# A fourth block product in each gate and up group, and three low parts made by an accumulating DMA

## The chip, the cores and the metric

The kernel runs on one core of one Trainium2 chip. The metric is device time in microseconds of one execution. The core's engines work side by side and wait for each other on semaphores: TensorE (PE) multiplies matrices into PSUM, VectorE (DVE) and ScalarE (ACT) work element by element, GpSimd (POOL) does small side work and issues a few DMAs, and SyncE (SP) issues the loads of the weights.

## The reference, cut to what matters

The model has two layers over a residual stream of 256 tokens and 2048 features. Each layer is a normed mixer and then a normed SwiGLU feed-forward network, and a last norm ends it. All weights and data are float32. The change lies in the feed-forward network:

```python
FFN_HIDDEN = -(-(8 * D_MODEL) // (3 * 256)) * 256      # 5632

def swiglu(xn, w_gate, w_up, w_down):
    return (jax.nn.silu(xn @ w_gate) * (xn @ w_up)) @ w_down
...
        h = h + swiglu(rms_norm(h, norm_ffn[layer]), w_gate[layer], w_up[layer], w_down[layer])
```

So `xn` is 256 x 2048, gate and up are 2048 x 5632 each, and down is 5632 x 2048.

## The kernel before, in words

Every float32 operand `a` is split into a high part `hi`, rounded to float32r, and a low part `lo = a - hi`. A product is three matmuls into one PSUM bank: high by high, high by low, low by high (`three`, lines 350 to 353, or lines 173 to 175 in the plain loop). A weight tile has 128 rows of k and 512 columns. Two k rows of tiles make a *pair* and are loaded with one DMA of 512 KB into a `raw` tile (`load_raw`, line 94, all on SP's queue, in order). `split_chunk` (line 147) then makes `hi` with a cast on ACT (line 150) and `lo` with a subtraction on DVE (line 151). `hi` and `lo` are rings of 6 buffers, the plain `raw` tiles a ring of 4. PE thus consumes a chunk of 512 KB in 2 (k rows) x 2 (blocks of 128 tokens) x 3 = 12 matmuls.

The feed-forward network (`ffn`, line 419) walks over the 5632 hidden columns in 11 *groups* of 512, in three *blocks* of 3, 4 and 4 groups (`PARTS`). A group computes gate and up for its 512 columns over all 2048 rows of k, that is 8 pairs, then the gated product, then four transposes per token block into `pf` (line 450), which give the left operand of down. After each block, the part of down that needs these columns is computed and added to the residual stream.

`pair_group` (line 358) computes a group for two matrices at once. `ORDER` gives its 8 pairs in sequence; a 0 marks a *plain* pair, a 1 a *block product*. A plain pair is 4 half products for each matrix, 24 matmuls, from two chunks (gate, then up). A block product takes the 2 x 2 blocks (two token blocks by two k rows, and two k rows by two matrices) with seven products in place of eight, 21 matmuls. It needs sums of the left operand, made beforehand while x is split (`sums_of`, line 208, called from `split_scaled` for every pair in `mixed_of(ORDER)`), and sums of the weights: four differences `t4` (lines 386 to 389, DVE), which are split into `ht` (ACT) and `lt` (DVE) in two halves (line 397). It also needs gate's chunk split (`hg`, `lg`) and the second row of up split (`hu`, `lu`, line 392). Four of the seven products go to four `prod` banks, shared by all block products of the group; three go straight to the plain banks. At the end of the group DVE combines the `prod` banks into `c` (lines 412 to 416) and adds the plain banks (line 438).

The buffers of a block product: `raw` tiles of the pool `fp`, two (one for gate, one for up); `t4`, one; `ht` and `lt`, two each, and both are used by one product. In `ORDER` of before, the three block products of a group are the pairs 2, 3 and 6, with a plain pair between any two.

The program is written in the order of the mathematics, but a scheduler that works when the program is built decides the order in which each engine gets its instructions. On the chip each engine then runs its list strictly in order. The same `pair_group` computes down, with the orders in `DOWN`.

Of the kernel before, what the change touches and what calls it, by code (L numbers as in the profile page):

```python
# [7 lines left out]
F32 = mybir.dt.float32  # L8
F32R = mybir.dt.float32r
AF = mybir.ActivationFunctionType  # L10
ALU = mybir.AluOpType
# [4 lines left out]
P = 128  # L16
# [5 lines left out]
NB = 512  # L22
CK = 2
# [7 lines left out]
OFF_QM, OFF_KM, OFF_VM, OFF_OM = 1536, 2048, 2560, 3584  # L31
CAP = 15.0
FILL = 24
ORDER = ((0, 0), (0, 1), (1, 2), (0, 4), (1, 3), (0, 5), (1, 6), (0, 7))
DOWN = {
    6: ((0, 0), (0, 1), (1, 2), (0, 3), (0, 4), (0, 5)),
    8: ((0, 0), (0, 1), (1, 2), (0, 3), (0, 4), (1, 5), (0, 6), (0, 7)),
# [11 lines left out]
def trunk(  # L49
# [20 lines left out]
    nc = tc.nc  # L70
# [7 lines left out]
    wr = ctx.enter_context(tc.tile_pool(name="wr", bufs=4))  # L78
# [12 lines left out]
    gn = [cp.tile([2 * KT, P], F32, name=f"gn{i}") for i in range(2)]  # L91
    nc.scalar.dma_start(gn[0], norm_mix.rearrange("l (k p) -> (l k) p", p=P))

    def load_raw(w, k0, c0, n, pool=wr):
        raw = pool.tile([P, CK, NB], F32, tag="raw", name="raw")
        nc.sync.dma_start(
            raw[:, :, 0:n], w[k0 * P : (k0 + CK) * P, c0 : c0 + n].rearrange("(k p) n -> p k n", p=P)
        )
        return raw
# [5 lines left out]
    for n in range(4):  # L105
# [7 lines left out]
        out=ident, in_=ident, pattern=[[-1, P]], compare_op=ALU.not_equal, fill=1.0, base=0, channel_multiplier=1  # L113
# [5 lines left out]
        out=upper, in_=ones, pattern=[[1, P]], compare_op=ALU.is_ge, fill=0.0, base=0, channel_multiplier=-1  # L119
# [20 lines left out]
    gain_columns(0)  # L140


    def load_chunk(w, k0, c0, n):
        raw = ahead.pop(0) if ahead else load_raw(w, k0, c0, n)
        return split_chunk(raw, n)

    def split_chunk(raw, n):
        hi = wp.tile([P, CK, NB], F32R, tag="hi", name="hi")
        lo = wp.tile([P, CK, NB], F32R, tag="lo", name="lo")
        nc.scalar.copy(hi[:, :, 0:n], raw[:, :, 0:n])  # L150
        nc.vector.tensor_tensor(  # L151
            out=lo[:, :, 0:n], in0=raw[:, :, 0:n], in1=hi[:, :, 0:n].bitcast(F32), op=ALU.subtract
        )
        return hi, lo
# [34 lines left out]
    sums = {}  # L189
# [55 lines left out]
    def split_plain(dst_h, dst_l, src):  # L245
        nc.scalar.copy(dst_h, src)  # L246
        nc.vector.tensor_tensor(out=dst_l, in0=src, in1=dst_h.bitcast(F32), op=ALU.subtract)  # L247
# [107 lines left out]
    def bank(par, name):  # L355
        return pm.tile([P, NB], F32, tag="pm", name=name) if par else pa.tile([P, NB], F32, tag="acc", name=name)

    def pair_group(fp, par, lhs, sums, mats, order):
        plain = [[bank(par, "acc") for _ in range(NT)] for _ in range(2)]
        prods = None  # L360
        kinds = [kind for kind, _ in order]
        t0, t1 = slice(0, P), slice(P, 2 * P)
        for pos, (kind, pair) in enumerate(order):
            k0 = 2 * pair
            if not kind:
                last = pos == len(order) - 1
                walk = [(i, t) for i in range(CK) for t in range(NT)]
                if last:
                    walk.sort(key=lambda it: it[1])
                for m, (w, c0) in enumerate(mats):  # L370
                    hi, lo = load_chunk(w, k0, c0, NB)
                    for i, t in walk:
                        ah, al = lhs(k0 + i)
                        ts = slice(t * P, (t + 1) * P)
                        three(
                            plain[m][t], ah[:, ts], al[:, ts], hi[:, i, :], lo[:, i, :],
                            pos == 0 and i == 0, last and i == CK - 1,
                        )
                continue
            first, last = 1 not in kinds[:pos], 1 not in kinds[pos + 1 :]  # L380
            if first:
                prods = [bank(1 - par, "prod") for _ in range(4)]
            ra, rb = (load_raw(w, k0, c0, NB, fp) for w, c0 in mats)
            hg, lg = split_chunk(ra, NB)
            t4 = fp.tile([P, 4, NB], F32, tag="t4", name="t4", bufs=1)
            nc.vector.tensor_tensor(out=t4[:, 0, :], in0=rb[:, 0, :], in1=ra[:, 0, :], op=ALU.subtract)
            nc.vector.tensor_tensor(out=t4[:, 1, :], in0=rb[:, 1, :], in1=rb[:, 0, :], op=ALU.subtract)
            nc.vector.tensor_tensor(out=t4[:, 2, :], in0=rb[:, 1, :], in1=t4[:, 0, :], op=ALU.subtract)
            nc.vector.tensor_tensor(out=t4[:, 3, :], in0=ra[:, 1, :], in1=t4[:, 2, :], op=ALU.subtract)
            hu = wp.tile([P, CK, NB], F32R, tag="hi", name="hi")  # L390
            lu = wp.tile([P, CK, NB], F32R, tag="lo", name="lo")
            split_plain(hu[:, 1, :], lu[:, 1, :], rb[:, 1, :])
            ht, lt = [], []
            for i in range(2):
                hs = fp.tile([P, 2, NB], F32R, tag="ht", name="ht")
                ls = fp.tile([P, 2, NB], F32R, tag="lt", name="lt")
                split_plain(hs, ls, t4[:, 2 * i : 2 * i + 2, :])
                ht += [hs[:, 0, :], hs[:, 1, :]]
                lt += [ls[:, 0, :], ls[:, 1, :]]
            sh, sl = sums(pair)  # L400
            xa, la = lhs(k0)
            xb, lb = lhs(k0 + 1)
            three(prods[0], xa[:, t0], la[:, t0], hg[:, 0, :], lg[:, 0, :], first, last)
            three(plain[0][0], xb[:, t0], lb[:, t0], hg[:, 1, :], lg[:, 1, :], False, False)
            three(plain[1][0], sh[:, 3, :], sl[:, 3, :], hu[:, 1, :], lu[:, 1, :], False, False)
            three(prods[1], sh[:, 0, :], sl[:, 0, :], ht[0], lt[0], first, last)
            three(prods[2], sh[:, 2, :], sl[:, 2, :], ht[1], lt[1], first, last)
            three(prods[3], sh[:, 1, :], sl[:, 1, :], ht[2], lt[2], first, last)
            three(plain[0][1], xb[:, t1], lb[:, t1], ht[3], lt[3], False, False)
        c = fp.tile([P, 4, NB], F32, tag="c", name="c", bufs=1)  # L410
        u2 = fp.tile([P, NB], F32, tag="tmp", name="u2")
        nc.scalar.copy(c[:, 0, :], prods[0])
        nc.vector.tensor_tensor(out=u2, in0=prods[3], in1=c[:, 0, :], op=ALU.add)
        nc.vector.tensor_tensor(out=c[:, 1, :], in0=prods[2], in1=u2, op=ALU.add)
        nc.vector.tensor_tensor(out=c[:, 2, :], in0=prods[1], in1=u2, op=ALU.add)
        nc.vector.tensor_tensor(out=c[:, 3, :], in0=prods[1], in1=c[:, 1, :], op=ALU.add)
        return plain, c

    def ffn(layer, fp, sx, sd, key, idx_next=None, key_next=None, finish=None):
# [6 lines left out]
        for g0, g1 in zip(PARTS, PARTS[1:]):  # L426
            end = g1 == PARTS[-1]
            nk = 4 * (g1 - g0)
            order = DOWN[nk // 2]
            for g in range(g0, g1):  # L430
                par = (g1 - 1 - g) % 2
                plain, c = pair_group(
                    fp, par, x_of, sums_x, [(w_gate[layer], g * NB), (w_up[layer], g * NB)], ORDER
                )
                for m in range(2):
                    for t in range(NT):
                        o = c[:, 2 * m + t, :]
                        nc.vector.tensor_tensor(out=o, in0=plain[m][t], in1=o, op=ALU.add)
                for t in range(NT):
                    nc.scalar.activation(c[:, t, :], c[:, t, :], AF.Silu, scale=r[:, t : t + 1])  # L440
                for t in range(NT):
                    nc.vector.scalar_tensor_tensor(
                        out=c[:, t, :], in0=c[:, 2 + t, :], scalar=r[:, t : t + 1], in1=c[:, t, :], op0=ALU.mult, op1=ALU.mult
                    )
                for half in range(2):
                    pt = bank(par, "pf").rearrange("p (i q) -> p i q", i=2)
                    for i in range(2):
                        cs = (2 * half + i) * P
                        for t in range(NT):
                            nc.tensor.transpose(pt[:, i, t * P : (t + 1) * P], c[:, t, cs : cs + P], ident)  # L450
                    pair = 2 * (g - g0) + half
                    k = 2 * pair
                    split_plain(mh[:, k : k + 2, :], ml[:, k : k + 2, :], pt)
                    if pair in mixed_of(order):
                        j = mixed_of(order).index(pair)
                        sums_of(
                            fp, sd[0][:, j, :, :], sd[1][:, j, :, :], lambda full, pt=pt: nc.scalar.copy(full, pt)
                        )
# [55 lines left out]
    with tc.tile_pool(name="ev", bufs=1) as ev:  # L514
# [3 lines left out]
            out=dist, in_=dist, pattern=[[-1, S]], compare_op=ALU.is_ge, fill=-NEG, base=P, channel_multiplier=1  # L518
        )
        nc.gpsimd.affine_select(  # L520
            out=dist, in_=dist, pattern=[[1, S]], compare_op=ALU.is_ge, fill=-NEG, base=-1, channel_multiplier=-1
# [4 lines left out]
            out=future, in_=future, pattern=[[1, P]], compare_op=ALU.is_ge, fill=-NEG, base=0, channel_multiplier=-1  # L526
# [126 lines left out]
        with tc.tile_pool(name="mp", bufs=1) as mp:  # L653
            dt_ = mp.tile([P, ML_H, NT, P], F32, name="dt_")
            for g in range(2):
                pb = pm.tile([P, 2, NT, P], F32, tag="pm", name="pb")
                for i in range(2):
# [7 lines left out]
                    op=ALU.add,  # L665
# [257 lines left out]
```

## Time and profile before

| | us |
|---|---|
| median of three runs | 2155.24 |
| lowest and highest | 2154.97 and 2155.56 |
| the profiled execution, its own time | 2154.99 |
| its span, first to last instruction | 2153.3 |
| DMA: moved in the span | 408.37 MB, mean 190 GB/s |

The profile is that of one execution. Its page gives each engine's busy time, the chain of work that ended last (followed back from the last instruction to what released it), the groups of instructions with their count, busy time and mean duration in ns, and what ended the idle time before them, and the DMA issues with the median time from issue to landing. Other views list instructions in order of time, the waits by who waited for whom (total us, times, longest us), and the busy time of each engine in a given stretch. `128x1024` means 128 partitions by 1024 elements. L150 is line 150 of the kernel. Durations of matmuls overlap, since they are pipelined: their starts are what counts. The granted clock of PE was 0.998 of full speed over the whole execution.

### The profile page before, as it was taken

To read this page: it belongs to the slowest core of one execution; us is meant where nothing else is said; L and a number is where in the kernel's file an instruction comes from. 1 tells how busy PE (TensorE), PEld (TensorE's weight loads), DVE (VectorE), ACT (ScalarE), POOL (GpSimd) and SP (SyncE) were. 2 spreads that over 40 slices of the span, in tenths; PEclk is the share of its full clock that TensorE was granted. 3 is DMA by queue.
4 is the path that set the end of the run, shared out by engine and by line. 5 is a ranking of instruction groups with operands and counts; after the bars stand their busy time and mean duration, and the time that the engine had idled before them with its cause. 6 is when DMAs were issued, how large, how long until landed. Compare 5 with 4: busy or idle time off the path is not lost.

```text
span 2153.3 us, 27002 instructions
## 1 busy us (share of the span) xinstructions
PE 2137.1 (99%) x9932; PEld 1774.6 (82%) x9932; DVE 1668.7 (77%) x2136; ACT 1164.1 (54%) x1514; POOL 37.7 (2%) x61
## 2 busy tenths in 40 slices
PE   8999999999999999999999999999999999999998
PEld 7888888888888888888888888888888888888886
DVE  6665567898889988998755555668988898888984
ACT  6564455655555545655545444555655555555553
POOL 2010000000000000000010000000000000000000
PEclk9999999999999999999999999999999999999999
DMA  8444555656665666656575554656556566656563
GB/s 266 147 157 145 169 171 191 208 194 203 203 201 180 210 195 205 200 191 196 160 234 166 166 177 149 212 176 205 195 192 206 190 200 209 196 199 203 178 213 127
DMA packets 213541, 408.37 MB, mean 190 GB/s; under 512 B 12736, under 2 KB 21024, under 8 KB 213152
## 3 DMA queue, kind: packets, MB, share of 16 engines
q1 hardware_dynamic: 212736, 402.90, 58.3%
q0 software_dynamic: 624, 3.72, 0.5%
q8 instruction: 78, 1.28, 0.2%
q14 instruction: 55, 0.45, 0.1%
q10 hardware_dynamic: 48, 0.02, 0.0%
HBM read 404.48 MB, written 2.11 MB: 189 GB/s over the span
## 4 chain that ended last, share of the span: by engine, by line
PE 98%; ACT 1%; issue 0%; DMA 0%; DVE 0%; DVEq 0%; POOLq 0%; POOL 0%; ACTq 0%
PE acc L353 17%; PE acc L352 17%; PE acc L351 17%; PE acc L173 10%; PE acc L175 10%; PE acc L174 10%; PE prod L353 4%; PE prod L352 4%; PE prod L351 4%; PE pf L450 1%; PE pt L224 1%; PE p L275 1%; PE ptm L258 1%; PE po L326 1%; PE pp L318 0%
## 5 line engine op out<-in xcount | busy, mean ns | idle before, releaser
L150 ACT CAST hi<-raw 128x1024 fp32r<-128x1024 f32 (+1 forms) x692 | 707.5, 1033 | 648.5 <-PE acc L353 314.3
L151 DVE TENSOR_TENSOR lo<-raw,hi 128x1024 fp32r<-128x1024 f32 (+1 forms) x692 | 825.7, 1201 | 288.1 <-ACT hi L150 285.9
L352 PE MATMUL acc<-lo,xh 128*128 128x512 f32 x946 | 368.4, 389 | 0.0
L353 PE MATMUL acc<-hi,xl 128*128 128x512 f32 x946 | 367.5, 391 | 0.0
L351 PE MATMUL acc<-hi,xh 128*128 128x512 f32 x946 | 365.2, 389 | 0.0
L173 PE MATMUL acc<-hi,xh 128*128 128x512 f32 (+3 forms) x736 | 276.8, 377 | 0.7 <-ACT hi L150 0.7
L175 PE MATMUL acc<-hi,xl 128*128 128x512 f32 (+3 forms) x736 | 276.9, 377 | 0.0
L174 PE MATMUL acc<-lo,xh 128*128 128x512 f32 (+3 forms) x736 | 276.4, 375 | 0.0
L247 DVE TENSOR_TENSOR lt<-t,ht 128x1024 fp32r<-128x1024 f32 x168 | 200.1, 1219 | 28.8 <-ACT ht L246 27.8
L246 ACT CAST ht<-t 128x1024 fp32r<-128x1024 f32 x168 | 174.6, 1053 | 81.1 <-PE prod L353 44.3
L352 PEld LDWEIGHTS acc<-lo,xh 128*128 128x128 f32 x946 | 177.6, 188 | 37.0
L353 PEld LDWEIGHTS acc<-hi,xl 128*128 128x128 f32 x946 | 177.6, 188 | 36.3
L351 PEld LDWEIGHTS acc<-hi,xh 128*128 128x128 f32 x946 | 177.7, 188 | 36.1
L352 PE MATMUL acc<-lo,mh 128*128 128x512 f32 x514 | 200.4, 390 | 0.0
L353 PE MATMUL acc<-hi,ml 128*128 128x512 f32 x514 | 199.4, 389 | 0.0
L351 PE MATMUL acc<-hi,mh 128*128 128x512 f32 x514 | 198.9, 389 | 0.0
L173 PEld LDWEIGHTS acc<-hi,xh 128*128 128x128 f32 x736 | 139.0, 189 | 24.9 <-ACT hi L150 1.1
L175 PEld LDWEIGHTS acc<-hi,xl 128*128 128x128 f32 x736 | 139.1, 189 | 24.4 <-issue 0.8
L174 PEld LDWEIGHTS acc<-lo,xh 128*128 128x128 f32 x736 | 139.1, 189 | 24.0 <-issue 0.7
L173 PE MATMUL acc<-hi,mh 128*128 128x512 f32 x320 | 125.8, 393 | 1.2 <-ACT mh L246 1.2
L174 PE MATMUL acc<-lo,mh 128*128 128x512 f32 x320 | 125.7, 393 | 0.0
L175 PE MATMUL acc<-hi,ml 128*128 128x512 f32 x320 | 124.0, 390 | 0.0
(299 smaller groups left out, 2726.8 us busy)
## 6 DMA issues: line engine op xcount, KB each, us to landing
raw<-in_w_gate_dram SPq DMA_DIRECT2D x176, 512.0 KB, 3.8
raw<-in_w_up_dram SPq DMA_DIRECT2D x176, 512.0 KB, 4.4
raw<-in_w_down_dram SPq DMA_DIRECT2D x176, 512.0 KB, 4.3
raw<-in_w_in_odd_dram SPq DMA_DIRECT2D x88, 512.0 KB, 3.8
raw<-in_w_in_even_dram SPq DMA_DIRECT2D x64, 512.0 KB, 4.2
raw<-in_w_out_even_dram SPq DMA_DIRECT2D x32, 512.0 KB, 3.7
raw<-in_w_out_odd_dram SPq DMA_DIRECT2D x32, 512.0 KB, 4.0
raw<-in_w_in_odd_dram SPq DMA_DIRECT2D x8, 272.0 KB, 2.8
```

The source lines that it names most:

```text
L150: nc.scalar.copy(hi[:, :, 0:n], raw[:, :, 0:n])
L151: nc.vector.tensor_tensor(out=lo[:, :, 0:n], in0=raw[:, :, 0:n], in1=hi[:, :, 0:n].bitcast(F32), op=ALU.subtract)
L173: nc.tensor.matmul(o, ah[:, ts], hi, start=(k == 0), stop=False)
L174: nc.tensor.matmul(o, ah[:, ts], lo, start=False, stop=False)
L175: nc.tensor.matmul(o, al[:, ts], hi, start=False, stop=(k == k_all - 1))
L224: nc.tensor.transpose(pt[:, i, t, :], h[:, t, k * P : (k + 1) * P], ident)
L246: nc.scalar.copy(dst_h, src)
L247: nc.vector.tensor_tensor(out=dst_l, in0=src, in1=dst_h.bitcast(F32), op=ALU.subtract)
L258: nc.tensor.transpose(pt[:, i, :], s_, ident)
L351: nc.tensor.matmul(o, ah, hi, start=start, stop=False)
L352: nc.tensor.matmul(o, ah, lo, start=False, stop=False)
L353: nc.tensor.matmul(o, al, hi, start=False, stop=stop)
```

## The change

1. `ORDER` marks four pairs in place of three: 2, 3, 5 and 6. Pairs 0, 1, 4 and 7 stay plain. Block products 2 and 3 follow each other directly, and so do 5 and 6.
2. `BY_DMA = (1, 4, 7)`: in these plain pairs, the low part of up's chunk (the second of the pair's two) is no longer made by DVE. ACT writes `-hi` into `lo`, and GpSimd issues a DMA that adds `raw` to it in place. These are 3 of the 8 plain chunks of a group.
3. The two `raw` tiles of a block product become one tile `r4` of four rows, gate's two and up's two, in a ring of one. The first two of the four differences become one instruction of 1024 elements.
4. The sums of the left operand are made for one pair more (through `mixed_of(ORDER)`), and their tiles `sx` grow by 4 KB a partition; the scratch of the DMAs that GpSimd issues shrinks from 8192 to 4096 bytes.

Line numbers of the changed kernel are 5 to 7 higher: the subtraction of line 151 is line 157, the negation and the DMA are lines 154 and 155, the differences are lines 394 to 396, the splits of line 246 and 247 are lines 252 and 253, and the load of line 96 is line 98.

```diff
-ORDER = ((0, 0), (0, 1), (1, 2), (0, 4), (1, 3), (0, 5), (1, 6), (0, 7))
+ORDER = ((0, 0), (0, 1), (1, 2), (1, 3), (0, 4), (1, 5), (1, 6), (0, 7))
+BY_DMA = (1, 4, 7)
...
+    def split_chunk(raw, n, by_dma=False):
         hi = wp.tile([P, CK, NB], F32R, tag="hi", name="hi")
         lo = wp.tile([P, CK, NB], F32R, tag="lo", name="lo")
         nc.scalar.copy(hi[:, :, 0:n], raw[:, :, 0:n])
+        if by_dma:
+            nc.scalar.mul(lo, hi.bitcast(F32), -1.0)
+            nc.gpsimd.dma_start(lo.bitcast(F32), raw, accum_op=ALU.add)
+            return hi, lo
...
-                    hi, lo = load_chunk(w, k0, c0, NB)
+                    hi, lo = load_chunk(w, k0, c0, NB, by_dma=m == 1 and pair in by_dma)
...
-            ra, rb = (load_raw(w, k0, c0, NB, fp) for w, c0 in mats)
-            hg, lg = split_chunk(ra, NB)
+            r4 = fp.tile([P, 4, NB], F32, tag="r4", name="r4", bufs=1)
+            for m, (w, c0) in enumerate(mats):
+                load_raw(w, k0, c0, NB, r4[:, 2 * m : 2 * m + 2, :])
+            hg, lg = split_chunk(r4[:, 0:2, :], NB)
             t4 = fp.tile([P, 4, NB], F32, tag="t4", name="t4", bufs=1)
-            nc.vector.tensor_tensor(out=t4[:, 0, :], in0=rb[:, 0, :], in1=ra[:, 0, :], op=ALU.subtract)
-            nc.vector.tensor_tensor(out=t4[:, 1, :], in0=rb[:, 1, :], in1=rb[:, 0, :], op=ALU.subtract)
-            nc.vector.tensor_tensor(out=t4[:, 2, :], in0=rb[:, 1, :], in1=t4[:, 0, :], op=ALU.subtract)
-            nc.vector.tensor_tensor(out=t4[:, 3, :], in0=ra[:, 1, :], in1=t4[:, 2, :], op=ALU.subtract)
+            nc.vector.tensor_tensor(out=t4[:, 0:2, :], in0=r4[:, 2:4, :], in1=r4[:, 0:4:2, :], op=ALU.subtract)
+            nc.vector.tensor_tensor(out=t4[:, 2, :], in0=r4[:, 3, :], in1=t4[:, 0, :], op=ALU.subtract)
+            nc.vector.tensor_tensor(out=t4[:, 3, :], in0=r4[:, 1, :], in1=t4[:, 2, :], op=ALU.subtract)
...
-            split_plain(hu[:, 1, :], lu[:, 1, :], rb[:, 1, :])
+            split_plain(hu[:, 1, :], lu[:, 1, :], r4[:, 3, :])
...
-    nc = _bacc.Bacc("TRN2", target_bir_lowering=False, num_devices=1, dynamic_dma_scratch_size=8192)
+    nc = _bacc.Bacc("TRN2", target_bir_lowering=False, num_devices=1, dynamic_dma_scratch_size=4096)
```

More of the change, by code (lines that the diff above doesn't have):

```diff
@@ L92, in trunk, with load_raw @@
     nc.scalar.dma_start(gn[0], norm_mix.rearrange("l (k p) -> (l k) p", p=P))
-    def load_raw(w, k0, c0, n, pool=wr):
-        raw = pool.tile([P, CK, NB], F32, tag="raw", name="raw")
+    def load_raw(w, k0, c0, n, raw=None):
+        if raw is None:
+            raw = wr.tile([P, CK, NB], F32, tag="raw", name="raw")
         nc.sync.dma_start(
@@ L140, in trunk, with load_chunk @@
     gain_columns(0)
-    def load_chunk(w, k0, c0, n):
+    def load_chunk(w, k0, c0, n, by_dma=False):
         raw = ahead.pop(0) if ahead else load_raw(w, k0, c0, n)
-        return split_chunk(raw, n)
-    def split_chunk(raw, n):
+        return split_chunk(raw, n, by_dma)
+    def split_chunk(raw, n, by_dma=False):
         hi = wp.tile([P, CK, NB], F32R, tag="hi", name="hi")
@@ L356, in bank, with pair_group @@
         return pm.tile([P, NB], F32, tag="pm", name=name) if par else pa.tile([P, NB], F32, tag="acc", name=name)
-    def pair_group(fp, par, lhs, sums, mats, order):
+    def pair_group(fp, par, lhs, sums, mats, order, by_dma=()):
         plain = [[bank(par, "acc") for _ in range(NT)] for _ in range(2)]
@@ L432, in ffn @@
                 plain, c = pair_group(
-                    fp, par, x_of, sums_x, [(w_gate[layer], g * NB), (w_up[layer], g * NB)], ORDER
+                    fp, par, x_of, sums_x, [(w_gate[layer], g * NB), (w_up[layer], g * NB)], ORDER, BY_DMA
                 )
```

## The prediction

> **What bounds the kernel now.** I read the page first: the span, the engines' shares, the chain of work that ended last.
>
> ```profile
> span 2153.3 us, 27002 instructions
> PE 2137.1 (99%) x9932; PEld 1774.6 (82%) x9932; DVE 1668.7 (77%) x2136; ACT 1164.1 (54%) x1514; POOL 37.7 (2%) x61
> PE 98%; ACT 1%; issue 0%; DMA 0%; DVE 0%; DVEq 0%; POOLq 0%; POOL 0%; ACTq 0%
> ```
>
> The tensor engine (PE) is 98% of the chain, so every matmul that goes shortens the run, as long as its data come in time. Then I cut out the stage that is changed. A group is 512 columns of gate and up; its transposes into pf mark where one ends. Two neighbouring groups of layer 0, in the view of windows (stretch, PE, PEld, DVE, ACT, POOL busy, clock, DMA share, GB/s):
>
> ```profile
> 593.31:636.42 43.11, 43.11 (x195) 35.70 (x194) 38.42 (x47) 24.34 (x28) 0.00 (x0) 1.00 0.60 195
> 636.42:679.50 43.08, 43.08 (x195) 35.75 (x194) 40.39 (x53) 25.29 (x29) 0.00 (x0) 1.00 0.62 196
> ```
>
> PE is busy throughout at full clock, 43.1 us a group. The vector engine (DVE) is busy 38.4 to 40.4 of these 43.1: in this stage it is close behind. Who waits for whom shows how far ahead the data lie:
>
> ```profile
> ACT hi L150 <- PE acc L353: 314.3, 244, 4.8
> DVE t L386 <- DMA raw<-in_w_up_dram: 45.4, 30, 4.2
> SPq L96 <- DVE lo L247: 82.1, 53, 5.4
> SPq L96 <- DVE t L389: 55.1, 40, 6.0
> ```
>
> The scalar engine (ACT) waits for PE to free hi buffers, so plain data are ready early. But the block products are fed through a ring of one: their loads wait on SP until the last reader of the pair before (L389, L247) is done, and 30 times DVE then waits up to 4.2 us for that load. This loop, load, read, release, load, is what I follow.
>
> **The change part by part.** Matmuls. A plain pair takes 24 matmuls, a block product 21. From the timeline of PE, a block product's first matmul and the tenth:
>
> ```profile
> 563.61 0.39 PE L351 MATMUL prod<-hi,xh 128*128 128x512 f32 x1
> ...
> 565.65 0.39 PE L351 MATMUL prod<-ht,sx 128*128 128x512 f32 x1
> ```
>
> Nine steps in 2.04 us are 0.227 each. 22 groups x 3 x 0.227 = 15.0 us less, 0.68 a group: PE alone would need 42.4.
>
> DVE's work. Its timeline in a block product, and what lies around the loads:
>
> ```profile
> 562.54 1.22 DVE L151 TENSOR_TENSOR lo<-raw,hi 128x1024 fp32r<-128x1024 f32 x1
> 563.67 0.68 DVE L389 TENSOR_TENSOR t<-raw,t 128x512 f32<-128x512 f32 x1
> 564.42 0.37 SPq L96 DMA_DIRECT2D raw<-in_w_gate_dram  x1
> 570.96 0.69 DVE L386 TENSOR_TENSOR t<-raw 128x512 f32<-128x512 f32 x1
> 571.57 0.69 DVE L387 TENSOR_TENSOR t<-raw 128x512 f32<-128x512 f32 x1
> 572.17 0.68 DVE L388 TENSOR_TENSOR t<-raw,t 128x512 f32<-128x512 f32 x1
> 572.77 1.22 DVE L151 TENSOR_TENSOR lo<-raw,hi 128x1024 fp32r<-128x1024 f32 x1
> 573.91 0.69 DVE L389 TENSOR_TENSOR t<-raw,t 128x512 f32<-128x512 f32 x1
> ```
>
> Starts follow each other by 0.60 behind 512 elements ("short") and by 1.14 behind 1024 ("long"). A group loses five long low parts (two of the converted pair, three to the DMA), gains one product (four long, three short, with the two subtractions merged: 6.4), and the other three products save 0.07 each by the merge: -5.7 + 6.4 - 0.2 = +0.5. DVE would be busy some 40 of 42.4 us. That alone would still fit.
>
> ACT. The three negations are not in the trace; nearest is the cast of the same size:
>
> ```profile
> L150 ACT CAST hi<-raw 128x1024 fp32r<-128x1024 f32 x660 | 687.5, 1053 | 614.7 <-PE acc L353 307.5 <-PE acc L175 230.4 <-issue 38.0
> L246 ACT CAST ht<-t 128x1024 fp32r<-128x1024 f32 x168 | 174.6, 1053 | 81.1 <-PE prod L353 44.3 <-DVE t L387 10.8 <-PE acc L353 10.0
> L246 ACT CAST hi<-raw 128x512 fp32r<-128x512 f32 x84 | 52.3, 622 | 87.1 <-PE acc L353 68.0 <-issue 13.0 <-ACT ht L246 4.2
> ```
>
> 3 x 1.05 + (1.05 + 0.62 + 2.1 - 2.1) = 4.8 us on 24.3 to 25.3: hidden in ACT's idle time, at most 4.8 a group if it weren't.
>
> The loop of r4. Order and buffer decide. The new order puts products 2 and 3, and 5 and 6, next to each other (before, a plain pair stood between any two), and r4 is one buffer of four rows that is free only when all readers of both halves are done. So a group now makes four turns of load, read, release. I take each turn's reading from the changed program's order of DVE instructions, in a middle group, from the first that reads r4 to the last. Pair 2: 3 long, 8 short (five of them sums of the group before). Pair 3: 3 long, 4 short. Pair 5: 3 and 3. Pair 6: 4 and 3. Together 13 x 1.14 + 18 x 0.605 = 25.7 us, in which no next load can be under way. Behind each release SP issues 0.06 us later (L389 ends at 564.35, the gate load is issued at 564.42), and the landing is on the page:
>
> ```profile
> raw<-in_w_gate_dram SPq DMA_DIRECT2D x176, 512.0 KB, 3.8
> raw<-in_w_up_dram SPq DMA_DIRECT2D x176, 512.0 KB, 4.4
> DMA to landing us min/median/max: 2.7/4.0/12.8
> ```
>
> Pair 2 starts with the subtraction and needs both halves: 0.06 + 0.37 + 4.4 = 4.8. Pairs 3, 5 and 6 start with the low part of gate: 0.06 + 3.8 + a cast of 1.05 = 4.9. Four turns: 25.7 + 4.8 + 3 x 4.9 = 45.2 us, more than PE's 42.4. What the order can't tell is how long DVE stands inside a turn waiting for a cast of ht, which in turn waits for PE to free ht (two buffers, both used by each product). Bounds: nothing, or one cast of 1.05 in each turn, 4.2. I take 1.5, nearer to nothing, since other DVE work stands between most casts and their low parts: 46.7 a group, 3.6 more than the 43.1 of before. x 22 = +79 us.
>
> The order bears this out. Before, the first matmul on a lo stands over 6 matmuls behind the instruction that makes it in 773 of 776 cases, that on an lt in 140 of 168. After, 145 of 776 and 114 of 212 stand within 6, and 80 of 212 ht within 2: PE takes data as they appear.
>
> Ends of the blocks. The groups run in six blocks (3, 4 and 4, twice). In each, the first r4 is loaded during the stage before: 4.8 less. Behind the last, cast, low part and six matmuls are left, 1.05 + 1.14 + 1.4 = 3.6 more. 6 x (3.6 - 4.8) = -7.
>
> The accumulating DMA. No row shows one. Nearest are GpSimd's own transfers and a load:
>
> ```profile
> cb<-scratch POOLq DMA_DIRECT2D x1, 2048.0 KB, 9.5
> gf<-in_norm_final_dram POOLq DMA_DIRECT2D x1, 1024.0 KB, 5.0
> scratch<-negct POOLq DMA_DIRECT2D x1, 16.0 KB, 4.0
> ```
>
> Below, 4.0; above, the 12.8 of the slowest load. Each moves 0.5 MB and reads its target too, like 1 to 1.5 MB: I take 6. Three things queue behind it: PE's matmuls on that lo; on SP the reload of its raw buffer, with the r4 loads behind that; for pair 7, DVE's sums that need the finished bank. Pair 1's is issued, in the order, just before the turn of pair 2 starts reading, and pair 3's r4 load, behind the raw reload, waits for that turn's end anyway: 3 long and 8 short, 8.2 us of cover. Pair 7's goes out beside the r4 load of the next group, and the sums stand behind that load and the same turn, with 12 matmuls between: 4.8 + 8.2 - 2.7 = 10.3. So 6 costs nothing, and 12.8 costs 4.6 + 2.5 = 7.1 a group.
>
> It also shares the DMA engines, at 0.60 to 0.62 for 8.4 MB a group (195 GB/s x 43.1 us): 1.5 to 4.5 MB more would be 0.72 to 0.94. The Trainium skill (DMA: Bandwidth & Descriptors, "Issuing engines are not separate DMA queues") says that transfers of all issuers run on the same 16 engines and interleave, which speaks against the change: every 0.5 us by which landings got later would add 4 x 22 x 0.5 = 44 us to my sum, while by the row's landings it stays as it is. No row here shows the two together.
>
> The rest: two more sums of x (L208 on) in the out projection, where DVE has room; the smaller DMA scratch: nothing, at most the 3 us of one such chain.
>
> **Sum.** Made on the profiled execution, 2154.99 us (span 2153.3), 0.25 below the median of the runs: -15 and +94 (46.7 against 42.4) make +79; -7; 2155 + 72 = 2227 us.
>
> **Rivals.** 1: PE stays the bound. The changed matmuls come through and the loop hides: 2155 - 15 = 2140. For it: 98% of the chain, DVE at 40 of 42.4. Against it: it needs turns 3 us shorter a group than their own instructions and loads; at the fastest landing, 2.7, four turns come to 45.2 - 3 x 1.1 - 1.7 = 40.2, so it decides there.
>
> 2: The accumulating DMA is the slow one. From 8.2 us on it holds up pair 3's r4 load, from 10.3 also DVE's sums; at 12.8 that is 22 x 7.1 = 156: 2383 us. For it: the slowest landing of a load, a target that is read as well, the same engines. Against it: 5.0 for 1 MB from the same queue.
>
> 3: Gain and loss cancel: four turns of 43.1 instead of 46.7, 2155.
>
> **How the numbers follow.** The forecast has 0.69; its own range runs from no waits in a turn (45.2: +46, with the ends 2194) to 4.2 of them (49.4: +139, without credit for the ends 2294). Rival 1 has 0.11, rival 2 0.17, rival 3 0.03. 2227 is the likeliest's. The range 2175 to 2320 leaves out rivals 1 and 3 and the upper part of 2. About 0.2% is what a measurement can tell from no change: faster 0.11, same 0.03, slower 0.86.
>
> **What would show it.** If right: the pf transposes of middle groups stand 46 to 48 us apart, matmuls still 0.227; PE's share falls to some 95%; the chain takes in the casts and low parts of ht and the loads of r4; L394 waits for r4's DMA over 60 times; PE idles before ht (L252) and lt (L253). The accumulate (L155) lands within 8 us. Wrong in the step of the loop: groups 42.4 apart. Wrong in the accumulate: landings over 8.2, and PE and SP waiting for it. Matmuls other than 66 fewer would void the first term.

## The result and the profile after

The changed kernel takes 2428.45 us (median of four runs, 2424.69 to 2434.2), before 2155.1 us beside it: a ratio of 1.127, 95% interval 1.124 to 1.130. The forecast of 2227 had the direction right and the size wrong, and the time lies above its range.

The page of the changed kernel: the span, the engines' busy time, the chain that ended last by engine, and the DMA issues with their median landing.

```profile
span 2423.0 us, 26943 instructions
PE 2245.4 (93%) x9866; PEld 1783.0 (74%) x9866; DVE 1679.9 (69%) x2106; ACT 1254.1 (52%) x1630; POOL 94.1 (4%) x127
...
PE 51%; DMA 22%; DVE 14%; issue 9%; ACT 4%; SPq 0%; DVEq 0%; POOLq 0%; ACTq 0%; POOL 0%
...
r<-in_w_gate_dram SPq DMA_DIRECT2D x88, 512.0 KB, 4.9
r<-in_w_up_dram SPq DMA_DIRECT2D x88, 512.0 KB, 5.8
...
lo<-raw POOLq DMA_DIRECT2D x66, 512.0 KB, 8.5
```

PE was 98% of the chain; it is 51% now, and transfers (22%) and DVE (14%) have taken its place. The 66 matmuls are gone (9866 against 9932), yet PE is busy 108 us longer. The trace shows `r4` as `r`. Who waited for whom (total us, times, longest), first SP's queue, then the engines:

```profile
SPq L98 <- DMA lo<-raw: 318.6, 66, 9.6
SPq L98 <- DVE t L396: 195.8, 47, 9.7
```

```profile
ACT hi L152 <- DMA r<-in_w_gate_dram: 201.9, 66, 7.1
...
PEld acc L358 <- DMA lo<-raw: 88.7, 27, 5.8
...
PE acc L358 <- DMA lo<-raw: 77.0, 25, 5.4
...
DVE t L394 <- DMA r<-in_w_up_dram: 52.3, 14, 5.2
```

Both the loop and the accumulate show. ACT stands 202 us for loads of `r4`, and SP's queue waits 66 times and PE 25 times for one of the 66 accumulates. Not as foretold is who waits for `r4`: the differences (L394) do so 14 times in place of over 60, and the cast of gate's half in front of them (L152) 66 times. The same groups as before, in the view of windows (stretch, PE, PEld, DVE, ACT, POOL busy, clock, DMA share, GB/s):

```profile
651.00:705.80 54.80, 48.87 (x191) 35.60 (x190) 39.81 (x47) 28.11 (x32) 2.55 (x3) 0.94 0.63 187
705.80:760.70 54.90, 48.34 (x189) 35.30 (x188) 40.82 (x51) 29.31 (x34) 2.56 (x3) 0.94 0.61 179
```

A group takes 55 us in place of 43. DVE does the 40 to 41 us that were forecast, but it does them with gaps. I take the loop of `r4` through the second of these groups: the issue of each gate load on SP, and the first DVE instruction that reads what it brought (start, us).

```profile
702.39 0.37 SPq L98 DMA_DIRECT2D r<-in_w_gate_dram  x1
...
713.64 0.37 SPq L98 DMA_DIRECT2D r<-in_w_gate_dram  x1
...
729.49 0.37 SPq L98 DMA_DIRECT2D r<-in_w_gate_dram  x1
...
740.81 0.37 SPq L98 DMA_DIRECT2D r<-in_w_gate_dram  x1
...
756.96 0.41 SPq L98 DMA_DIRECT2D r<-in_w_gate_dram  x1
```

```profile
707.71 1.22 DVE L157 TENSOR_TENSOR lo<-r,hi 128x1024 fp32r<-128x1024 f32 x1 [1.69 <-ACT hi L152]
...
721.61 1.23 DVE L157 TENSOR_TENSOR lo<-r,hi 128x1024 fp32r<-128x1024 f32 x1 [2.47 <-ACT hi L152]
...
734.35 1.23 DVE L157 TENSOR_TENSOR lo<-r,hi 128x1024 fp32r<-128x1024 f32 x1 [2.51 <-ACT hi L152]
...
748.45 1.23 DVE L394 TENSOR_TENSOR t<-r 128x1024 f32<-128x1024 f32 x1 [2.52 <-DMA r<-in_w_up_dram]
```

Four turns, 756.96 - 702.39 = 54.6 us: that is the group. From issue to first reading 5.3, 8.0, 4.9 and 7.6, together 25.8; the other 28.8 are reading and its waits. Counted in the same way, from pair 2 to pair 6, the ten groups that are neither first nor last of their block have 29.4 us of loads and 27.9 of reading in the mean. The long second load stands beside an accumulate. SP's and GpSimd's issues there, and PE:

```profile
711.78 0.86 POOL L155 DMA_DIRECT2D lo<-raw  x1 [19.16 <-ACT lo L154]
```

```profile
711.84 0.37 SPq L98 DMA_DIRECT2D raw<-in_w_gate_dram  x1
...
714.06 1.59 SPq L98 DMA_DIRECT2D r<-in_w_up_dram  x1
719.57 0.37 SPq L98 DMA_DIRECT2D raw<-in_w_up_dram  x1
```

```profile
714.96 0.40 PE L359 MATMUL prod<-ht,sx 128*128 128x512 f32 x1
719.56 0.80 PE L358 MATMUL acc<-lo,xh 128*128 128x512 f32 x1 [4.20 <-DMA lo<-raw]
720.15 0.63 PE L359 MATMUL acc<-hi,xl 128*128 128x512 f32 x1
720.58 0.63 PE L358 MATMUL acc<-lo,xh 128*128 128x512 f32 x1
721.00 0.63 PE L359 MATMUL acc<-hi,xl 128*128 128x512 f32 x1
```

The accumulate is issued at 711.78 and lets go at 719.5, 7.7 us later: PE's next low part starts at 719.56, and SP's reload of that raw tile at 719.57. Behind the stall PE's steps are 0.42 to 0.43 us in place of 0.227.

By the order of issue, three to a group, this accumulate is pair 4's, which stands between products 3 and 5. Of the 77.0 us that PE waits for accumulates, 52.6 (19 times) are for pair 4's and 24.4 (6 times) for pair 7's; for pair 1's it never waits. SP waits for all three alike: 113, 102 and 103 us.

Where the 273 us lie follows from the pf transposes. The 16 distances between neighbouring groups of a block sum to 698.2 us before and 899.4 after: 201 us, 12.6 a group. The other 69 of the 270 us between the spans lie outside these distances, for example 116.1 in place of 102.9 us between the last group of a block and the first of the next.

### The profile page after: what moved, and what is told of

Read it like the earlier page. It is cut to its first block, busy times and chain, and to the rows that moved or that the text cites. A ratio compares the mean times of both kernels' runs of the same rounds, so it can differ in the third digit from the quotient of the medians.

```text
span 2423.0 us, 26943 instructions
## 1 busy us (share of the span) xinstructions
PE 2245.4 (93%) x9866; PEld 1783.0 (74%) x9866; DVE 1679.9 (69%) x2106; ACT 1254.1 (52%) x1630; POOL 94.1 (4%) x127
## 4 chain that ended last, share of the span: by engine, by line
PE 51%; DMA 22%; DVE 14%; issue 9%; ACT 4%; SPq 0%; DVEq 0%; POOLq 0%; ACTq 0%; POOL 0%
PE acc L179 9%; PE acc L180 9%; PE acc L181 9%; DMA r<-in_w_gate_dram 7%; DMA lo<-raw 7%; PE acc L358 6%; PE acc L359 6%; DMA r<-in_w_up_dram 5%; PE acc L357 5%; DVE lo L157 3%; DMA r<-in_w_down_dram 3%; DVE t L394 3%; ACT hi L152 2%; DVE t L396 2%; DVE t L395 1%
## 5 line engine op out<-in xcount | busy, mean ns | idle before, releaser
L152 ACT CAST hi<-raw 128x1024 fp32r<-128x1024 f32 (+3 forms) x564 | 567.9, 1026 | 458.3 <-PE acc L181 251.9
L157 DVE TENSOR_TENSOR lo<-raw,hi 128x1024 fp32r<-128x1024 f32 (+3 forms) x498 | 588.2, 1190 | 260.2 <-ACT hi L152 259.2
L357 PE MATMUL acc<-hi,xh 128*128 128x512 f32 x792 | 318.9, 411 | 17.9 <-DVE c L421 12.6
L253 DVE TENSOR_TENSOR lt<-t,ht 128x1024 fp32r<-128x1024 f32 x212 | 254.9, 1220 | 61.2 <-ACT ht L252 61.0
L157 DVE TENSOR_TENSOR lo<-r,hi 128x1024 fp32r<-128x1024 f32 x106 | 129.6, 1223 | 168.0 <-ACT hi L152 168.0
L152 ACT CAST hi<-r 128x1024 fp32r<-128x1024 f32 x106 | 111.1, 1048 | 254.4 <-DMA r<-in_w_gate_dram 201.9
L357 PE MATMUL acc<-hi,mh 128*128 128x512 f32 x514 | 199.8, 393 | 19.4 <-DVE u L420 16.0
L358 PE MATMUL acc<-lo,mh 128*128 128x512 f32 x514 | 201.9, 393 | 0.9 <-DVE lo L157 0.6
L359 PE MATMUL acc<-hi,ml 128*128 128x512 f32 x514 | 199.9, 391 | 0.0
L394 DVE TENSOR_TENSOR t<-r 128x1024 f32<-128x1024 f32 x106 | 129.3, 1220 | 67.3 <-DMA r<-in_w_up_dram 52.3
L180 PEld LDWEIGHTS acc<-lo,xh 128*128 128x128 f32 x736 | 139.1, 189 | 23.9 <-issue 0.7
```

Source lines behind the costliest of these rows:

```text
L157: nc.vector.tensor_tensor(out=lo[:, :, 0:n], in0=raw[:, :, 0:n], in1=hi[:, :, 0:n].bitcast(F32), op=ALU.subtract)
L180: nc.tensor.matmul(o, ah[:, ts], lo, start=False, stop=False)
L357: nc.tensor.matmul(o, ah, hi, start=start, stop=False)
L358: nc.tensor.matmul(o, ah, lo, start=False, stop=False)
L359: nc.tensor.matmul(o, al, hi, start=False, stop=stop)
L394: nc.vector.tensor_tensor(out=t4[:, 0:2, :], in0=r4[:, 2:4, :], in1=r4[:, 0:4:2, :], op=ALU.subtract)
```

## The experiments

Each time is a median, each ratio is to the kernel before in the same series (2154 to 2155 us), with its 95% interval.

### Undoing one part, doing one part alone

**four_no_dma.** `BY_DMA = (1, 4, 7)` becomes `BY_DMA = ()`.

> The changed kernel with the accumulating DMA taken out: all low parts on DVE again, four block products, one r4. Theory A (the accumulate is most of the loss: PE waits for it, and the loads beside it land 2 to 3 us later, 6.1 and 7.9 us for the two halves of r4 in place of 3.7 and 4.6): the loop of r4 is left as I forecast it, 25.7 us of reading, up to 3.4 us more for the low parts that come back to DVE, 19.5 of loads and 1.5 of waits, 46.7 to 50.1 us a group, 2227 to 2300 us in all; the PE clock goes back to nearly 1.0. Theory B (the accumulate is hidden, the loop of r4 is the whole loss): 2400 to 2450, no better than the changed kernel, since DVE has 3.4 us more to do a group.

2348.0 us, 1.089 (1.087 to 1.091). Between the theories: taking the DMA out gives 80 us back, but 193 stay, 48 more than the top of what the forecast's loop allowed. So the loop without any accumulate was mis-sized too. Its ten middle groups, counted as above, have 23.6 us of loads and 28.1 of reading, so it is the loads that the accumulate makes longer.

**three_with_dma.** The kernel before, with this added to `split_chunk` and its callers:

```diff
+        if by_dma:
+            nc.scalar.mul(lo, hi.bitcast(F32), -1.0)
+            nc.gpsimd.dma_start(lo.bitcast(F32), raw, accum_op=ALU.add)
+            return hi, lo
```

> The kernel before with the accumulating DMA alone: three block products in the old order, two raw tiles, low parts of up's chunk of pairs 1, 4 and 7 by DMA. Theory A: PE stands for the accumulates and the loads beside them land later; in the changed kernel the matmuls and weight loads wait 166 us for them in all, so 2155 + 80 to 200, 2235 to 2355. Theory B: hidden, 2150 to 2165, with 3.4 us less DVE work a group.

2188.9 us, 1.015 (1.014 to 1.017): +34. Not hidden, but less than theory A asked for.

**four_two_raw.** As four_no_dma, but the load of before, and the four differences as four instructions again:

```diff
-            r4 = fp.tile([P, 4, NB], F32, tag="r4", name="r4", bufs=1)
-            for m, (w, c0) in enumerate(mats):
-                load_raw(w, k0, c0, NB, r4[:, 2 * m : 2 * m + 2, :])
...
+            ra, rb = (
+                load_raw(w, k0, c0, NB, fp.tile([P, CK, NB], F32, tag="raw", name="raw")) for w, c0 in mats
+            )
...
```

> As the run without the DMA, but with the two raw tiles of before in place of r4, and the four differences unmerged. Theory A and the loop as forecast (each half is free only behind the difference that reads it last, so the two tiles let go at almost the same time): within 25 us of the run without the DMA. Rival C (the ring of one r4 is what makes the loop, its two halves freed together): 40 us or more below the run without the DMA.

2276.2 us, 1.057 (1.055 to 1.058), 72 below four_no_dma: rival C's side. Two tiles are better than one, and still 121 us slower than before. That they are freed one by one is the likely reason; the run doesn't show it by itself.

**three_r4.** The changed kernel with the old `ORDER` and `BY_DMA = ()`.

> Three block products in the old order, no DMA, but r4 and the merged difference. Both theories let a plain pair stand between any two block products, so the turn has time: 2150 to 2165. Rival C (r4 is the loss whatever the order): 2180 or more.

2170.2 us, 1.007 (1.005 to 1.008): +15, a little above the range. With three products the one tile is nearly affordable; with four it is not.

### Is it the neighbours, or the sum of the turns?

**spread_r4** and **spread_two_raw.** four_no_dma and four_two_raw with another order:

```diff
-ORDER = ((0, 0), (0, 1), (1, 2), (1, 3), (0, 4), (1, 5), (1, 6), (0, 7))
+ORDER = ((0, 0), (1, 2), (0, 1), (1, 3), (0, 4), (1, 5), (1, 6), (0, 7))
```

> Four block products, one r4, no DMA, but the order changed so that a plain pair stands in front of products 2, 3 and 5 (0, product 2, 1, product 3, 4, products 5 and 6, 7). Theory L (the loop: what counts is the sum of four turns of reading and loading in one buffer, whatever stands between on PE): four turns took 27 us of reading and 24 of loads without the DMA, so some 50 us a group still, 2300 to 2350. Theory N (neighbours: only a product directly behind another is late): one such pair in place of two, half of the 193 us, 2235 to 2270.

> The same order with the two raw tiles and no DMA. Theory L: as four block products in the order of the change with two raw tiles, 2276, within 25 us. Theory N: 2195 to 2230, half of 121 us. If DVE's own work is the bound (some 44 us a group): 2175 to 2190.

2381.1 us, 1.105 (1.103 to 1.107), and 2279.3 us, 1.058 (1.057 to 1.060). Spreading the products helps in neither; with one `r4` it is 33 us slower than the order of the change, 31 above theory L's range. Its ten middle groups have 23.9 us of loads (23.6 in four_no_dma). So it is not the neighbours that make the loss, as far as this one other order shows.

**four_r4x2** and its control **before_five.** The run without the DMA, with room for two:

```diff
-    wp = ctx.enter_context(tc.tile_pool(name="wp", bufs=6))
+    wp = ctx.enter_context(tc.tile_pool(name="wp", bufs=5))
...
-            r4 = fp.tile([P, 4, NB], F32, tag="r4", name="r4", bufs=1)
+            r4 = fp.tile([P, 4, NB], F32, tag="r4", name="r4", bufs=2)
```

> The run of four block products without the DMA, with two buffers of r4 in place of one (the space comes from hi and lo, 5 buffers each in place of 6). Theory L (the loop through one buffer is the loss): the loads run while the pair before is still read, so DVE's own work is left as the bound, 46.5 us a group by that run's windows against 43.6 before: 2155 + 22 x 2.9 = 2219, in 2180 to 2240. Rival E (DVE in order is the loss: casts and differences that wait for each other inside a product): 2300 to 2350, no change from one buffer.

> Control: the kernel before with 5 buffers of hi and lo in place of 6. ACT waits for PE to free hi there, so data lie a chunk less ahead: 2155 to 2170 by every theory. What it is above 2155 belongs to the 5 buffers and is to be taken off the runs with two r4.

2208.9 us, 1.025 (1.023 to 1.026), and for the control 2155.7 us, 1.0002 (0.9993 to 1.0012). This is the run that settles the loop: the second buffer takes 139 of 193 us away, and the 5 buffers that go with it cost nothing in the control. What is left is in the main DVE's own work. Its windows, a middle group of four_no_dma and one of four_r4x2:

```profile
683.70:734.50 50.80, 45.56 (x189) 33.66 (x188) 43.91 (x54) 26.57 (x32) 0.00 (x0) 1.00 0.48 166
```

```profile
649.00:696.00 47.00, 43.55 (x189) 33.92 (x187) 44.26 (x54) 25.78 (x32) 0.00 (x0) 1.00 0.53 177
```

DVE's 44 us are the same; with two buffers they fill 94% of the group, with one 86%.

**four_r4x2_dma.** The changed kernel with these two edits.

> The changed kernel, DMA included, with two buffers of r4 (and 5 of hi and lo). Theory L and A together: the loop gone, DVE at 42 us a group fits under PE, and the accumulates are left: PE waits for them and the loads beside them, as in three products with the DMA (+34): 2155 - 15 + 34 + the cost of 5 buffers, 2170 to 2200. If the transfers are the larger part (A alone, 80 us): 2220 or more.

2242.3 us, 1.041 (1.039 to 1.043), above the first range and in the second. The loop gone, the accumulating DMA still makes it 33 us slower, about as with three products. It takes 3.4 us of work a group from DVE, the bound of four_r4x2, so it should have been faster: what it costs eats that saving as well.

### What the accumulate costs by itself

**three_copy_unread** and **three_accumulate_unread.** In three products and with DVE still making every low part, GpSimd moves the same chunks into a tile that nothing reads, once as a copy, once as an accumulate (there with a memset of that tile at the start):

```diff
+        if by_dma:
+            nc.gpsimd.dma_start(spare, raw)
```

```diff
+    nc.gpsimd.memset(spare, 0.0)
...
+            nc.gpsimd.dma_start(spare, raw, accum_op=ALU.add)
```

> The kernel before with three transfers more a group and all low parts still on DVE: GpSimd copies the raw chunk of up of pairs 1, 4 and 7 into a spare tile that nothing reads. Only the shared DMA engines and the later release of raw are left of the accumulate. If the +34 of three products with the accumulating DMA come from the sharing and from raw being held: 2175 to 2195. If they come from PE waiting for the low part itself: 2155 to 2165.

> As the unread copy beside the kernel before (2154.7), but the three transfers a group add raw to the spare tile in place of copying it; all low parts still on DVE. Theory S (sharing: an accumulate holds the engines twice as long as a copy, 8.2% of the span against 4.2% for 66 of them, and the loads beside it get late): 2175 to 2195. Theory W (PE waiting for the low part is the cost): 2153 to 2160.

2154.7 us, 0.9999 (0.9990 to 1.0009), and 2163.2 us, 1.004 (1.003 to 1.005). The first lies just below all that was expected, the second a little above theory W's range; but its 8 us are not the DMA: its distances between groups are those of before to 0.1 us, and PE waits 6.9 us once at the start for `ident`, which GpSimd makes behind the new memset. So neither transfer costs anything beside loads that have slack, nor does the smaller DMA scratch of 4096 bytes, which both runs have. Yet the accumulate holds the engines longer. The software queue's packets, MB and share of the 16 engines, copy and then accumulate (0.5% in the kernel before):

```profile
q0 software_dynamic: 10128, 38.33, 4.7%
```

```profile
q0 software_dynamic: 10128, 38.33, 9.4%
```

For the same bytes 8.9% against 4.2%, twice the time. The Trainium skill (Collectives: The Full Stack, "The bandwidth ceiling: the fold count and why AG ≠ RS ≠ AR") says that ReduceScatter's add needs two source reads and so pushes twice the traffic of a copy. For the accumulating DMA of this kernel these rows agree.

**three_copy_read.** three_with_dma without `accum_op`, so that the low part of these chunks is raw itself.

> As three products with the accumulating DMA (2189), but the DMA copies raw into lo in place of adding it, so that the low part of these three chunks is raw itself: PE waits for the same transfer in the same place, and it lands earlier (4.9 us in the median of the unread copies, 6.8 the accumulates). Theory W: 2165 to 2180, part of the 34 us left by the shorter landing. Theory S: 2153 to 2160.

2155.5 us, 1.0003 (0.9994 to 1.0012). A copy in the same place, waited for by the same instructions, lands after 4.0 us in the median (the accumulate: 6.8) and costs nothing, which theory W didn't expect. What costs is the slower transfer that something waits for. PE waits for it hardly at all in three_with_dma; SP does, and DVE behind it. The waits of SP and DVE in three_with_dma, then DVE's in three_copy_read:

```profile
SPq L97 <- DMA lo<-raw: 359.5, 62, 11.0
```

```profile
DVE t L391 <- DMA raw<-in_w_up_dram: 120.6, 55, 4.8
```

```profile
DVE t L391 <- DMA raw<-in_w_up_dram: 74.4, 36, 4.4
```

The kernel before has 45.4 us for the last kind. So I read the waits as follows: the accumulate keeps its raw tile, SP stands at the reload of that tile, and the loads of the next block product stand behind SP. At the end of the chain PE waits 13.1 us for DVE's sums at the end of a group (`u` and `c`), which it does neither in the kernel before nor in three_copy_read. The next run tests the part of the queue.

**three_dma_six_raw.** three_with_dma with `bufs=5` for hi and lo and `bufs=6` for raw.

> Three block products with the accumulating DMA (2189), with 6 raw tiles in place of 4 (the space from 5 buffers of hi and lo in place of 6, which alone cost nothing). If the cost goes through SP's queue (reloads of raw held by the accumulate, block loads behind them): DVE's wait for the block products' up load falls from 121 us to some 45, 2150 to 2170. If it is the accumulates' share of the engines or PE's own wait: still 2180 to 2195.

2174.2 us, 1.010 (1.007 to 1.012). SP's wait for accumulates falls to 209.5 us and 15 of the 34 us go; DVE's wait for the up load does not fall, it is 171.4. So the reading is borne out in part only: the raw ring carries 15 of the 34 us, while DVE's wait, which should have fallen with them, rose. How the other 19 come about stays open.

**four_two_raw_dma** and **four_copy_read.** The changed kernel with the two raw tiles, and the changed kernel with a copy in place of the accumulate.

> The changed kernel with the two raw tiles of before in place of r4, DMA included; without the DMA it is 2276. If the DMA costs the same 33 us everywhere (two r4, three products): 2300 to 2320. If it costs more where the loads of a loop are the bound, as with one r4 (80): 2330 to 2370.

> The changed kernel with the DMA copying raw into lo in place of adding it (the low part of these three chunks is raw itself). Three products: accumulate +34, copy 0. If the accumulate's own engine time and landing are the cost here too: below the run without the DMA (2348), since DVE has 3.4 us less to do a group and 27 us of reading and 24 of loads are left, 2270 to 2340. If any 0.5 MB beside the loads of r4 costs that much: 2390 to 2430.

2421.1 us, 1.124 (1.123 to 1.126), and 2370.8 us, 1.101 (1.099 to 1.103). The first is above both ranges: with the DMA, the two raw tiles lose their advantage, since it costs 145 us there. And where the loads are in the loop even a copy is not free: 23 us above four_no_dma with less work on DVE, between the two guesses.

### Versions that could have won

**four_pool_sub** and **spread_two_raw_pool.** The three low parts as a subtraction on GpSimd:

```diff
-            nc.scalar.mul(lo, hi.bitcast(F32), -1.0)
-            nc.gpsimd.dma_start(lo.bitcast(F32), raw, accum_op=ALU.add)
+            nc.gpsimd.tensor_tensor(out=lo, in0=raw, in1=hi.bitcast(F32), op=ALU.subtract)
```

> The changed kernel with the three low parts made by a subtraction on GpSimd in place of the negation and the accumulating DMA: the DVE work of the changed kernel without its transfers. If the 80 us between the changed kernel and the one without the DMA are the transfers (A), and the 3.4 us a group that DVE saves count in the loop: 2270 to 2340, below the run without the DMA (2348). If a GpSimd subtraction is as late for PE as the DMA was (over 8 us), or holds up DVE: 2380 to 2450.

> Four block products in the spread order, two raw tiles, the three low parts on GpSimd. The candidate for the gain of 15 us: if DVE's work is the bound once the neighbours are apart, DVE is back at 40 of 42.4 us and the time is 2140 to 2160; by theory L (two turns through one pair of tiles) still 2220 to 2280.

2415.7 us, 1.1215 (1.1198 to 1.1232), and 2351.0 us, 1.091 (1.089 to 1.092): 68 and 72 us slower than with the low parts on DVE. The second lies above everything that was expected.

**first_group_four.** four_r4x2 with four products in the first group of each block and three in the old order elsewhere.

> No DMA, two r4, 5 buffers of hi and lo; four block products only in the first group of each of the six blocks, three in the old order in the others. If DVE has room there, with the stage before to work ahead: 6 x 0.68 = 4 us less, 2149 to 2153. If DVE's 46.5 us of work show in that group too: 6 x 3, 2160 to 2175.

2156.0 us, 1.0004 (0.9995 to 1.0013): no difference, and between the two guesses. The second group of each block then comes 42.7 us behind the first, and the next block's first group 108.8 us behind the last, against 43.1 and 102.9 before: what is won inside is given back between the blocks. No version tried beats the kernel before.

## Why the prediction was wrong

**Matmuls and DVE's work: right.** 66 matmuls fewer, 0.227 us each where PE runs at full clock; DVE 40 to 41 us in the two groups shown, as summed, and the 44 us without the DMA follow from the same durations.

**The loop of r4: the mechanism right, the size not.** A turn is load, read, release, and four of them set the group; four_r4x2 shows it. The failing term is the load: 19.5 us for four were forecast, the quoted group has 25.8, the ten middle groups 29.4 in the mean, and 23.6 even in four_no_dma, where no accumulate runs. Were all 22 groups like these, that would be 218 and 90 us. Reading with its waits, 25.7 + 1.5 forecast, is 27.9 and 28.1; that the guess of 1.5 hit so well is luck. The loads were priced at the median landing of all gate and up loads of the kernel before (3.8 and 4.4 us), 110 of each 176 of them plain. In a tight loop the release lets several out together: between 740.81 and 741.95 SP issues both halves of `r4` and a raw tile, and an accumulate goes out at 741.65. The halves land after a median of 4.9 and 5.8 us, in four_no_dma after 4.2 and 5.3. There the halves with no load of a raw tile beside them (under way at their issue, or issued within 2 us) land after 3.8 and 4.7 us, those with three or more after 6.1 and 7.0.

**The ends of the blocks: wrong in sign.** Taken at -7, they cost 8 us in four_no_dma (spans less distances, by the same count as above) and 69 in the changed kernel. The count is rough: the distance that ends with a block's last group holds 52 to 56 of down's matmuls in four_no_dma, 47 or 48 in the changed kernel and 35 or 36 before, so that some of what the ends cost stands among the distances.

**The accumulating DMA: the term put at nothing.** It was taken at 6 us, covered up to 8.2 for pair 1's and 10.3 for pair 7's. It lands after 4.5 to 11.1 us, 8.5 in the median: pair 1's 8.2, pair 4's 6.7, pair 7's 10.2. So the first passes its cover in 12 of 22 cases and the last in 9. For pair 4's the prediction worked out no cover at all, and that is the one for which PE stands most, 52.6 us. Taking the DMA out gives 80 of the 201 us back by which the forecast was too low; 121 stay with the loop, in a run whose DVE makes three low parts more a group. 60 of the 73 us between the spans of four_no_dma and the changed kernel lie outside the 16 distances, 51 of them between the last group of a block and the first of the next: PE's idle time there is 41 us in place of 12, and 21 of it are waits for accumulates. Within the 16 distances (886.3 us without it, 899.4 with it) the cost is 13: PE waits 52 us for accumulates there, but its idle time grows only from 93 to 112, since it stands there for the loop anyway. That a block's first group has no such slack in which to hide an accumulate was not counted; it is my reading of these waits, and no run tries it alone.

**The sharing of the engines.** The rule cited from the Trainium skill (DMA: Bandwidth & Descriptors, "Issuing engines are not separate DMA queues") held in this kernel: loads of `r4` with an accumulate under way land after 6.1 us (gate) and 7.9 (up) in the median, 3.7 and 4.6 without one, by their records in the trace. That is 2.4 to 3.3 us, where I had priced 0.5 and then left it out. Some of it is the crowd of other loads: with one load of a raw tile beside them in both cases it is 6.2 against 4.1 and 7.3 against 5.3, some 2 us. But three_accumulate_unread shows that it costs only where a load is waited for: gate and up loads land after 5.0 us there with an accumulate under way, 4.5 without, and the groups keep their distances.

**The range took the two costs apart.** Rival 2 put the slow accumulate on top of the loop, 2227 + 156 = 2383, and came nearest. But its 156 us stood on a landing of 12.8 us in every case, where the longest is 11.1, and its loop was the forecast's, 121 us short of four_no_dma: being near is luck in part. The range left the upper part of rival 2 out; its upper end of 2320 holds the loop's longest waits (2294), but not these and a slow accumulate together. The loop makes every late transfer count, the accumulate makes transfers late: +34 or +33 us where no loop binds, +80 and +145 where one does. What stays open is how the 34 us of three products divide between SP's queue (15 by the one run) and the rest.

## What to carry to other kernels

A ring of one is a loop: add reading time and loading time over all its turns, with landings under the load that the loop itself makes, before counting the engines' busy shares; if the sum is near the bound, try a second buffer: here it took 139 us away, and another order none. Work handed to the DMA engines isn't free just because they are only 60% busy: ask who waits for its landing, which buffer it holds, and which queue stands behind that buffer. Two costs that feed each other are to be added in the upper end of a range, not offered as alternatives.

## What the hardware showed unexpectedly

**A stall of PE costs twice.** Behind the stall of 4.2 us quoted above PE goes on at half its rate for some 5 us (its steps are 0.23 again from 725.1): the granted clock is 0.51 from 719.5 to 725.0 and 1.00 from 725 to 735. Over the span it is 0.970 (0.998 before). Between neighbouring 512-column matmuls there are 394 steps of 0.36 to 0.50 us, 70 before; what they exceed 0.227 by sums to 77 us, 12 before. How much of these 65 us lies on the path that sets the end wasn't tried. The Trainium skill (TensorE: Matmul & The Clock Gate, "HAM oscillation — how this bites in real kernels") says that idle gaps over some 3.4 us set the clock back to half; the stall here and the steps behind it agree. But shorter gaps did it too: four_no_dma has twelve stretches at half clock inside the run with no idle gap of PE above 2.1 us near them, one at 508.6 us with three gaps of 0.98, 0.76 and 1.01 us within 4 us.

**GpSimd slows DVE.** In four_pool_sub a GpSimd subtraction of 1024 elements takes 2.4 us, and DVE's subtractions beside it take twice their time. The same low part of 512 elements in four_no_dma, then in four_pool_sub (count, busy us, mean ns):

```profile
L253 DVE TENSOR_TENSOR lo<-r,hi 128x512 fp32r<-128x512 f32 x106 | 72.7, 686 | 1.7 <-ACT hi L252 1.6
```

```profile
L252 DVE TENSOR_TENSOR lo<-r,hi 128x512 fp32r<-128x512 f32 x106 | 94.2, 889 | 1.2 <-ACT hi L251 1.2
```

Of the 106, the 35 that run beside a GpSimd subtraction take 1.31 us in the mean, the other 71 take 0.68. Of DVE's low parts of 1024 elements, 40 run beside one and take 2.48 us, the other 532 take 1.22.
